# Two of the seven half products of a weight tile summed by TensorE in one PSUM bank instead of by VectorE

## The chip, the cores and the metric

The kernel runs on one core of a Trainium2 chip. A core has five engines that each run their own queue of instructions in order: TensorE (PE, with its weight loads as PEld) for matmuls, VectorE (DVE), ScalarE (ACT), GpSimd (POOL) and SyncE (SP), which only starts transfers. They wait for each other by semaphores. Matmuls write into PSUM, which has eight banks; a bank holds 128 x 512 numbers in fp32. The metric is the device time of one execution in microseconds (us), lower is better; three runs of the kernel before gave 1572.64 to 1574.14 with a median of 1573.52.

## The reference

One block works on 512 latent tokens and 256 context tokens of 1024 channels: a SwiGLU feed-forward network (FFN), a token mixer, and a second FFN on the latent tokens alone. The change touches only the first matrix product of the two FFNs, `u @ wi`.

```
def swiglu(u, wi, wo):
    gate, up = jnp.split(u @ wi, 2, axis=-1)
    return (jax.nn.silu(gate) * up) @ wo

def ffn_half(t, m, s, nw, wi, wo):
    u = modulate(t, nw, m[3 * s], m[3 * s + 1])
    return t + 0.5 * m[3 * s + 2] * swiglu(u, wi, wo)
...
h = ffn_half(h, lat_m, 0, norm_w[l, 0], ffn1_wi[l], ffn1_wo[l])
hc = ffn_half(hc, ctx_m, 0, norm_w[l, 0], ffn1_wi[l], ffn1_wo[l])
...
h = ffn_half(h, lat_m, 2, norm_w[l, 2], ffn2_wi[l], ffn2_wo[l])
```

`wi` is 1024 x 5632 (two times 2816 hidden channels), all in fp32. The kernel splits each operand into a high part of reduced precision and the rest (names ending in h and l) and adds three matmuls, high times high, high times low and low times high.

## The kernel before, in words

A weight tile of `wi` is 1024 rows by 256 hidden channels. Its product with the tokens is cut in halves along all three sides, which would be eight products of half size, and is computed with seven (Strassen's scheme in Winograd's form): seven combinations of weight quarters times seven combinations of token quarters, and additions that put the four quarters of the result together. One call of `half_gemm` does this for one weight tile, with a column count N of 384 in the first FFN (768 tokens) and 256 in the second. In this document such a call is a **round**. A product is 12 matmuls (four blocks of 128 rows, three matmuls each) into one PSUM bank, so a round is 84 matmuls. Products are numbered 0 to 6 in their order.

Hidden channels are done in pairs of 128 (`half_pair`): a **gate round**, whose quarters go through Silu on ScalarE into the tiles `s`, and then an **up round**, whose quarters are multiplied into `s` by VectorE (line 1157); the finished `s` is split into `ah` and `al` (lines 76 and 77 in `split`) for the second matrix product. There are 20 rounds in the first FFN (from about 79 to 549 us) and 20 in the second (from about 1226 to 1523 us), numbered 1 to 40 here; odd rounds are gate rounds, even ones up rounds. The first pair of hidden channels of each FFN is done in another way.

After some pairs the second matrix product (`down`, the matmuls of line 229) is done for the hidden channels collected so far. It stands between the gate round and the up round of the next pair, so it cuts the rounds into **blocks**: rounds 1 to 3, 4 to 7, 8 to 11, 12 to 13, 14 to 17 and 18 to 20 in the first FFN, 21 to 27, 28 to 35 and 36 to 40 in the second.

What happens around a round:

- Weights come by DMA into `raw`; GpSimd forms four sums of weight quarters (`ws`, line 247: s3, s1, s2 and the fourth); each of the seven operands is split into `wh` by a cast on ScalarE and `wl` by a subtraction on VectorE. They go through a ring of 6 slots (8 in the second FFN), so a weight is prepared 6 or 8 products ahead, when a product sets a slot free.
- Product 0 is copied from its bank into SBUF by ScalarE (tile `hu`, line 307). VectorE then does seven additions (line 296), each of one bank and one tile in SBUF: product 0 plus product 1 is quarter (0,0) of the result; `hu` plus product 4, and so on for the other three quarters.
- The token operands are the normed tokens (`u_hi`, `ul_hi` and the like) and four sums of them, `T0` to `T3`.
- Every engine's order is fixed when the program is built: a scheduler orders the instructions by its own estimate of when each can run. On the chip an instruction that waits holds up all that stand behind it on its engine.

In the first FFN VectorE and ScalarE also do parts of another computation between the products (lines 511 to 600, the modulation by `w_ada`).

Of the kernel before, what the change touches and what calls it, by code (L numbers as in the profile page):

```python
# [12 lines left out]
AF = mybir.ActivationFunctionType  # L13
# [22 lines left out]
class Block:  # L36
# [203 lines left out]
    def half_items(self, w, r0, c0):  # L240

        nc, st = self.nc, {}
        a = lambda k, m: st["raw"][k][:, :, m * P : (m + 1) * P]

        def sub(x, y, op=ALU.subtract):
            t = self.sp.tile([P, 4, P], F32, tag="ws", name=self.n("ws"), bufs=self.sums)
            nc.gpsimd.tensor_tensor(out=t, in0=x, in1=y, op=op)  # L247
            return t

        def make(i):  # L250
            if i == 0:
                st["raw"] = self.load_raw([(w, r0, c0, 256)], KT)
                s3 = sub(a(0, 0), a(0, 1))
                s1 = sub(a(0, 1), a(1, 1), ALU.add)
                s2 = sub(s1, a(0, 0))
                st["w"] = [a(0, 0), a(1, 0), s3, sub(a(1, 0), s2), s2, a(1, 1), s1]
            src = st["w"][i]
            h, l = (t.rearrange("p (k n) -> p k n", k=4) for t in self.ring())
            self.split(h, l, src)
            return h, l  # L260

        return [(1, lambda i=i: make(i)) for i in range(7)]

    def half_operands(self, u):

        o = lambda k, t: lambda kt: u(k, t, kt)
        v = lambda j: lambda kt: self.T[j][kt]
        self.hx = [o(0, 0), o(1, 0), v(2), o(1, 1), v(1), v(3), v(0)]

    def half_sums(self, kt, x0, x1, last=None):  # L270

# [19 lines left out]
    def half_gemm(self, N, out, fill):  # L291

        nc = self.nc
        banks = []
        t = self.tmp.tile([P, N], F32, tag="hu", name=self.n("hu"), bufs=2)
        add = lambda o, x, y: nc.vector.tensor_tensor(out=o, in0=x, in1=y, op=ALU.add)  # L296
        for i in range(7):
            h, l = self.next_w()
            ps = self.small()[:, :N]
            banks.append(ps)  # L300
            for kt in range(4):
                xh, xl = self.hx[i](kt)
                for j in range(3):
                    nc.tensor.matmul(ps, (h, h, l)[j][:, kt, :], (xh, xl, xh)[j], start=kt == 0 and j == 0, stop=kt == 3 and j == 2)  # L304
            self.done_w()
            if i == 0:
                nc.scalar.copy(t, ps)
            elif i == 1:
                c = out(0, 0)
                add(c, t, ps)  # L310
                out(0, 0, c)
            elif i == 4:
                add(t, t, ps)
                c22, c12 = out(1, 1), out(0, 1)
                add(c22, t, banks[2])
                add(c12, t, banks[3])
            elif i == 5:
                c = out(1, 0)
                add(c, c22, ps)
                out(1, 0, c)  # L320
            elif i == 6:
                add(c12, c12, ps)
                out(0, 1, c12)
                add(c22, c22, ps)
                out(1, 1, c22)
            fill(i)
# [787 lines left out]
    def ffn(self, i, first, tail, fillers, after, between, tail_pool):  # L1114

        nc = self.nc
        ctx = i == 0
        W = TOK if ctx else SEQ
        N = W // 2
        bufs = max(k1 - k0 for k0, k1 in self.parts[i])  # L1120
        fill = lambda: next(fillers, None)
        acts, held = [], []

        def silu():
            return self.tmp.tile([P, W], F32, tag="s", name=self.n("s"), bufs=2 if ctx else 3)

        def keep(s):
            acts.append([self.act.tile([P, W], F32R, tag="a" + k, name=self.n("a" + k), bufs=bufs) for k in "hl"])
            self.split(*acts[-1], s)

        def evac_gate(pg):
            s = silu()
            for k, g in zip((0, SEQ), pg):
                w = min(SEQ, W - k)
                self.last_silu = nc.scalar.activation(s[:, k : k + w], g[:, :w], AF.Silu)
            return s

        def evac_up(s, pu):
            for k, u in zip((0, SEQ), pu):
                w = min(SEQ, W - k)  # L1140
                c = s[:, k : k + w]
                nc.vector.tensor_tensor(out=c, in0=c, in1=u[:, :w], op=ALU.mult)
            keep(s)

        def half_pair(m):
            ss = [silu(), silu()]
            at = lambda i, j: ss[i][:, j * N : (j + 1) * N]

            def gate(i, j, c=None):
                if c is not None:  # L1150
                    self.last_silu = nc.scalar.activation(c, c, AF.Silu)
                return at(i, j)

            def up(i, j, c=None):
                if c is None:
                    return self.tmp.tile([P, N], F32, tag="c", name=self.n("c"), bufs=3)
                nc.vector.tensor_tensor(out=at(i, j), in0=at(i, j), in1=c, op=ALU.mult)  # L1157
                if j == 1:
                    keep(ss[i])

            every = (1, 4) if m > 4 or not ctx else range(m == 2, 7)
            self.half_gemm(N, gate, lambda j: fill() if j in every and m > 2 else None)
            if held:
                held.pop()()
            self.half_gemm(N, up, lambda j: fill() if j in every else None)

        def down(acts, group, each, then=None):

            nk = len(acts)
            segs = []  # L1170
            for s, t0, w in group:
                sl = slice(s * SEQ + t0, s * SEQ + t0 + w)
                segs.append((sl.start, w, lambda kt, sl=sl: (acts[kt][0][:, sl], acts[kt][1][:, sl])))
            for t in range(4):
                w_ = self.next_w()
                os = [self.wide(W) for _ in range(2)]
                if t == 0:
                    self.gemm([(o, w_, j * P, P) for j, o in enumerate(os)], segs, nk)
                    if ctx and then:
                        then()  # L1180
                for j, o in enumerate(os):
                    m = 2 * t + j
                    if t:
                        self.gemm([(o, w_, j * P, P)], segs, nk)
                    for s, t0, w in group:
                        h = (self.h_l, self.h_c)[s][:, m, t0 : t0 + w]
                        nc.vector.scalar_tensor_tensor(out=h, in0=o[s][:, t0 : t0 + w], scalar=self.hg[:, s, m : m + 1],  # L1187
                                                       in1=h, op0=ALU.mult, op1=ALU.add)
                        each(m, s, t0, w)
                    fill()  # L1190
                self.done_w()
                if t == 0 and then and not ctx:
                    then()

        for k0, k1 in self.parts[i]:
            for m in range(k0, k1, 2):
                if m == 0:
                    first(evac_gate, evac_up)
                else:
                    half_pair(m)  # L1200
            if k1 < HM:
                held.append(lambda acts=tuple(acts): down(acts, [(0, 0, SEQ)] + ([(1, 0, CTX)] if ctx else []), lambda *k: None))
                acts.clear()
        for _ in fillers:
            pass
        self.log_exp(self.last_silu)
        tail_pool()
        then = None
        for group in tail:
            down(acts, [group], after, then)  # L1210
            then = lambda group=group: between(*group)
        then()
# [826 lines left out]
```

## Time and profile before

| | |
|---|---|
| median of three runs | 1573.52 us |
| the profiled execution, its own time | 1573.72 us |
| its span (first to last instruction) | 1571.9 us, so 1.8 us lie around it |
| mean granted TensorE clock | 0.994 |
| TensorE busy | 98% of the span |
| VectorE busy | 78% |
| ScalarE busy | 50% |
| GpSimd busy | 18% |

The spans and waits come from one profiled execution. A busy share is a mean over all stages; which engine is waited for in a stage is read from the waits and the timeline of that stage. The end of a matmul is modelled by the profiler, its start is measured.

### The profile page before, as it was taken

Reading aid. Unit: us, or ns where it says so; the run is one execution under the profiler, and the core shown is the slowest. Engines: PE = TensorE matmul, PEld = TensorE weight load, DVE = VectorE, ACT = ScalarE, POOL = GpSimd, SP = SyncE. Lnnn points to the kernel's source line nnn. Section 1 sums busy time; section 2 is a strip of 40 time slices with the busy share of each in tenths; the row PEclk is TensorE's granted clock in tenths of the full one; section 3 lists DMA queues with packets and bytes.
Section 4 is the critical chain, followed back from the end, with each engine's and each line's share of the span. In section 5 each row is a group of like instructions: output and inputs, shape, how many; then the busy total and the mean of one; then the engine's idle time right before and its main releaser. Section 6 shows DMA issues by size and latency. Waiting matters only on the chain. (4 is left out here: it accounts for less than half of the span.)

```text
span 1571.9 us, 24897 instructions
## 1 busy us (share of the span) xinstructions
PE 1536.4 (98%) x9292; PEld 1378.4 (88%) x9292; DVE 1229.4 (78%) x2230; ACT 779.4 (50%) x1363; POOL 281.8 (18%) x222
## 2 busy tenths in 40 slices
PE   8989999999999999999999999999999999999997
PEld 4778998999998988899898888878899898998997
DVE  5897999989996797776577577777756996797695
ACT  6754242433252456355353487778335643444365
POOL 0121212311312130000000100000013442451322
PEclk9999999999999999999999999999999999999999
DMA  9225334342443233121216223223531234234233
GB/s 329 89 68 154 101 115 128 112 137 66 136 128 94 81 105 108 41 58 52 66 54 188 74 61 93 68 81 121 174 108 55 68 104 125 81 95 132 83 116 113
DMA packets 165076, 163.63 MB, mean 104 GB/s; under 512 B 7618, under 2 KB 162524, under 8 KB 164956
## 3 DMA queue, kind: packets, MB, share of 16 engines
q1 hardware_dynamic: 163932, 159.68, 33.5%
q0 software_dynamic: 1024, 2.36, 0.5%
q8 instruction: 73, 1.20, 0.3%
q14 instruction: 47, 0.39, 0.1%
HBM read 159.89 MB, written 2.10 MB: 103 GB/s over the span
## 5 line engine op out<-in xcount | busy, mean ns | idle before, releaser
L76 ACT CAST wh<-raw 128x512 fp32r<-128x512 f32 x396 | 239.9, 618 | 240.6 <-PE sm L229 96.4
L77 DVE TENSOR_TENSOR wl<-raw,wh 128x512 fp32r<-128x512 f32 x396 | 288.7, 740 | 85.4 <-ACT wh L76 83.0
L229 PE MATMUL sm<-al,wh 128*128 128x512 f32 (+1 forms) x576 | 172.8, 340 | 0.1
L229 PE MATMUL sm<-ah,wh 128*128 128x512 f32 (+1 forms) x576 | 172.7, 342 | 0.0
L229 PE MATMUL sm<-ah,wl 128*128 128x512 f32 (+1 forms) x576 | 172.2, 339 | 0.0
L76 ACT CAST wh<-ws 128x512 fp32r<-128x512 f32 x160 | 97.9, 618 | 135.1 <-PE sm L229 65.5
L229 PE MATMUL mm<-ul_lo,wh 128*128 128x512 f32 x352 | 141.7, 402 | 0.0
L229 PE MATMUL mm<-ul_hi,wh 128*128 128x512 f32 x352 | 140.9, 400 | 0.0
L229 PE MATMUL mm<-ul_hi,wl 128*128 128x512 f32 x352 | 139.9, 397 | 0.0
L77 DVE TENSOR_TENSOR wl<-ws,wh 128x512 fp32r<-128x512 f32 x160 | 126.1, 799 | 10.9 <-ACT wh L76 10.6
L523 DVE SCALAR_TENSOR_TENSOR acc<-apiece,cs,acc 128x256 f32<-128x256 f32 x224 | 121.8, 567 | 14.9 <-DMA apiece<-in_w_ada_dram 12.6
L247 POOL TENSOR_TENSOR ws<-raw 128x512 f32<-128x512 f32 x40 | 61.1, 1529 | 357.8 <-DVE wl L77 141.0
L229 PEld LDWEIGHTS sm<-al,wh 128*128 128x128 f32 x576 | 98.5, 189 | 13.0 <-DVE al L77 0.3
L229 PEld LDWEIGHTS sm<-ah,wh 128*128 128x128 f32 x576 | 98.4, 188 | 12.9 <-ACT ah L76 0.3
L229 PEld LDWEIGHTS sm<-ah,wl 128*128 128x128 f32 x576 | 98.5, 189 | 12.8
L304 PE MATMUL sm<-u_lo,wh 128*128 128x384 f32 x320 | 108.0, 337 | 1.6 <-DVE u_lo L77 1.6
L304 PE MATMUL sm<-u_hi,wh 128*128 128x384 f32 x320 | 107.8, 337 | 0.1
L304 PE MATMUL sm<-u_hi,wl 128*128 128x384 f32 x320 | 107.8, 337 | 0.0
L1187 DVE SCALAR_TENSOR_TENSOR h_l<-sm,hg,h_l 128x512 f32<-128x512 f32 (+1 forms) x80 | 55.0, 692 | 44.3 <-PE sm L229 44.1
L1599 POOL DMA_DIRECT2D gwr<-in_lru_wr_dram x8 | 5.8, 726 | 417.2 <-PE mm L229 294.6
L229 PEld LDWEIGHTS mm<-ul_hi,wh 128*128 128x128 f32 x352 | 66.3, 188 | 15.8 <-issue 0.5
L229 PEld LDWEIGHTS mm<-ul_hi,wl 128*128 128x128 f32 x352 | 66.3, 188 | 15.3
(496 smaller groups left out, 4258.0 us busy)
## 6 DMA issues: line engine op xcount, KB each, us to landing
raw<-in_ffn_wi_dram SPq DMA_DIRECT2D x84, 512.0 KB
apiece<-in_w_ada_dram SPq DMA_DIRECT2D x112, 256.0 KB
raw<-in_ffn_wo_dram SPq DMA_DIRECT2D x48, 512.0 KB
raw<-in_w_in_dram SPq DMA_DIRECT2D x48, 512.0 KB
araw<-in_w_ada_dram SPq DMA_DIRECT2D x8, 1024.0 KB
raw<-in_w_in_dram SPq DMA_DIRECT2D x16, 256.0 KB
raw<-in_w_out_gla_dram SPq DMA_DIRECT2D x8, 512.0 KB
raw<-in_w_out_lru_dram SPq DMA_DIRECT2D x8, 512.0 KB
```

Of the source, the lines that this page charges most:

```text
L76: nc.scalar.copy(hi, src)
L77: rest = lambda: (nc.gpsimd if eng == "p" else nc.vector).tensor_tensor(out=lo, in0=src, in1=hi.bitcast(F32), op=ALU.subtract)
L229: ins = nc.tensor.matmul(dst[:cols, d0 : d0 + width], wk, xs, start=(kt == 0 and i == 0 and not (shared and n)), stop=(kt == kts - 1 and i ...
L247: nc.gpsimd.tensor_tensor(out=t, in0=x, in1=y, op=op)
L304: nc.tensor.matmul(ps, (h, h, l)[j][:, kt, :], (xh, xl, xh)[j], start=kt == 0 and j == 0, stop=kt == 3 and j == 2)
L523: nc.vector.scalar_tensor_tensor(out=acc[:, s, :], in0=raw[:, kt, :], scalar=c, in1=acc[:, s, :], op0=ALU.mult, op1=ALU.add)
L1187: nc.vector.scalar_tensor_tensor(out=h, in0=o[s][:, t0 : t0 + w], scalar=self.hg[:, s, m : m + 1], in1=h, op0=ALU.mult, op1=ALU.add)
L1599: nc.gpsimd.dma_start(out=raw[:, 0:2, :], in_=self.a["lru_wr"][0, :, blk].rearrange("d c e -> c d e"))
```

## The change

Products 1 and 2 change places: the sum s3 times T2 is now product 1, and the product of weight quarter (1,0) with token quarter (1,0), which was product 1, is now product 2. Product 2 doesn't start a bank of its own. Its matmuls add onto product 0 in that product's bank (`banks[0]`, no `start`), after ScalarE has copied product 0 to `hu`. The bank then holds quarter (0,0), which `out` takes straight from PSUM: in a gate round ScalarE's Silu reads the bank, in an up round VectorE's multiplication does. The addition of `i == 1` is gone, and six remain. A round now takes six banks from the pool instead of seven.

```
@@ half_items
-                st["w"] = [a(0, 0), a(1, 0), s3, sub(a(1, 0), s2), s2, a(1, 1), s1]
+                st["w"] = [a(0, 0), s3, a(1, 0), sub(a(1, 0), s2), s2, a(1, 1), s1]
@@ half_operands
-        self.hx = [o(0, 0), o(1, 0), v(2), o(1, 1), v(1), v(3), v(0)]
+        self.hx = [o(0, 0), v(2), o(1, 0), o(1, 1), v(1), v(3), v(0)]
@@ half_gemm
         for i in range(7):
             h, l = self.next_w()
-            ps = self.small()[:, :N]
+            ps = banks[0] if i == 2 else self.small()[:, :N]
             banks.append(ps)
             for kt in range(4):
                 xh, xl = self.hx[i](kt)
                 for j in range(3):
-                    nc.tensor.matmul(ps, (h, h, l)[j][:, kt, :], (xh, xl, xh)[j], start=kt == 0 and j == 0, stop=kt == 3 and j == 2)
+                    nc.tensor.matmul(ps, (h, h, l)[j][:, kt, :], (xh, xl, xh)[j], start=kt == 0 and j == 0 and i != 2,
+                                     stop=kt == 3 and j == 2, skip_group_check=i == 2)
             self.done_w()
             if i == 0:
                 nc.scalar.copy(t, ps)
-            elif i == 1:
-                c = out(0, 0)
-                add(c, t, ps)
-                out(0, 0, c)
+            elif i == 2:
+                out(0, 0, ps)
             elif i == 4:
                 add(t, t, ps)
                 c22, c12 = out(1, 1), out(0, 1)
-                add(c22, t, banks[2])
+                add(c22, t, banks[1])
                 add(c12, t, banks[3])
@@ half_pair, gate
-                    self.last_silu = nc.scalar.activation(c, c, AF.Silu)
+                    self.last_silu = nc.scalar.activation(at(i, j), c, AF.Silu)
```

The first place to look at is TensorE's order where product 2 begins, here in round 34 (an up round of the second FFN). `ul` are the tokens, `T2` the second token sum, the numbers tell tiles apart. Before, `sm_2901` is the bank of product 0, `sm_2904` that of product 1 and `sm_2908` that of product 2:

```order
L304 MATMUL sm_2904_14977<-ul_hi_6011,wh_2874_14828 128x256
L304 MATMUL sm_2904_14977<-ul_lo_6012,wh_2874_14828 128x256
L304 MATMUL sm_2904_14977<-ul_hi_6011,wl_2875_14829 128x256
L304 MATMUL sm_2908_14997<-T20h_12340,wh_2877_14846 128x256 [waits DVE_49,Activation_49]
L304 MATMUL sm_2908_14997<-T20l_12341,wh_2877_14846 128x256
L304 MATMUL sm_2908_14997<-T20h_12340,wl_2878_14847 128x256
```

Now `sm_2852` is the bank of product 0 and `sm_2855` that of product 1:

```order
L304 MATMUL sm_2855_14895<-T23h_12296,wh_2826_14748 128x256
L304 MATMUL sm_2855_14895<-T23l_12297,wh_2826_14748 128x256
L304 MATMUL sm_2855_14895<-T23h_12296,wl_2827_14749 128x256
L304 MATMUL sm_2852_14877<-ul_hi_5961,wh_2829_14766 128x256 [waits Activation_49]
L304 MATMUL sm_2852_14877<-ul_lo_5962,wh_2829_14766 128x256
L304 MATMUL sm_2852_14877<-ul_hi_5961,wl_2830_14767 128x256 [waits DVE_49]
```

Product 2 goes back to the bank of product 0, and its first matmul waits for ScalarE (Activation), which has to have read that bank. In seven of the 40 rounds the scheduler puts one or five matmuls of product 3 ahead of product 2; in the first three rounds and in round 21, where products of several banks are mixed, the mixture changes too. On SP's queue the same transfers stand, with those of weights and of `w_ada` interleaved differently in the first FFN.

The second place is ScalarE's order around the copy of product 0 in the same round. `s_2870` and `s_2871` are the Silu tiles of the gate round just before, `wh` are casts of weights for later products. Before:

```order
L1151 ACTIVATE s_2870_14812<-s_2870_14812 128x256 [waits DVE_49]
L76 CAST wh_2883_14882<-ws_2862_14792 128x512 [waits PE_49,Activation_49]
L76 CAST wh_2886_14899<-raw_2859_14786 128x512 [waits PE_49,Activation_49]
L76 CAST wh_2889_14919<-ws_2861_14790 128x512 [waits PE_49,Activation_49]
L1151 ACTIVATE s_2871_14813<-s_2871_14813 128x256 [waits DVE_49,Activation_49]
L76 CAST wh_2898_14950<-raw_2892_14938 128x512 [waits DMAHW0_49,PE_49]
L1151 ACTIVATE s_2870_14812<-s_2870_14812 128x256 [waits DVE_49]
L1151 ACTIVATE s_2871_14813<-s_2871_14813 128x256 [waits DVE_49]
L76 CAST wh_2902_14972<-raw_2893_14940 128x512 [waits DMAHW1_49,PE_49]
L307 COPY hu_2900_14958<-sm_2901_14959 128x256 [waits PE_49]
```

Now, with the line numbers of the changed kernel (Silu at 1150, the copy at 308):

```order
L1150 ACTIVATE s_2822_14732<-sm_2825_14735 128x256 [waits PE_49]
L76 CAST wh_2834_14800<-ws_2814_14712 128x512 [waits PE_49,Activation_49]
L76 CAST wh_2837_14817<-raw_2811_14706 128x512 [waits PE_49,Activation_49]
L76 CAST wh_2840_14837<-ws_2813_14710 128x512 [waits PE_49,Activation_49]
L1150 ACTIVATE s_2823_14733<-s_2823_14733 128x256 [waits DVE_49,Activation_49]
L76 CAST wh_2849_14868<-raw_2843_14856 128x512 [waits DMAHW0_49,PE_49]
L1150 ACTIVATE s_2822_14732<-s_2822_14732 128x256 [waits DVE_49]
L1150 ACTIVATE s_2823_14733<-s_2823_14733 128x256 [waits DVE_49]
L76 CAST wh_2853_14890<-ws_2845_14860 128x512 [waits PE_49,Pool_49]
L308 COPY hu_2851_14876<-sm_2852_14877 128x256 [waits PE_49]
```

The first Silu no longer waits for VectorE but for TensorE. The copy keeps its place behind the three Silus that wait for VectorE's additions of the round before, and the cast just ahead of it now waits for GpSimd's sum instead of a DMA. In gate rounds the copy stands behind one or both casts `ah<-s`, which wait for VectorE's multiplications, in both kernels.

The third place is VectorE's order at the same point. Before, the addition into `c_2907` is the one that goes, `hu_2900` is the copied product 0:

```order
L77 TENSOR_TENSOR wl_2903_14973<-raw_2893_14940,wh_2902_14972 128x512 [waits DMAHW1_49,PE_49,Activation_49]
L296 TENSOR_TENSOR c_2907_14994<-hu_2900_14958,sm_2904_14977 128x256 [waits PE_49,Activation_49]
L1157 TENSOR_TENSOR s_2870_14812<-s_2870_14812,c_2907_14994 128x256 [waits DVE_49]
L77 TENSOR_TENSOR wl_2906_14991<-ws_2894_14942,wh_2905_14990 128x512 [waits Activation_49]
L77 TENSOR_TENSOR wl_2910_15011<-ws_2897_14948,wh_2909_15010 128x512 [waits PE_49,Activation_49]
L77 TENSOR_TENSOR wl_2913_15028<-ws_2896_14946,wh_2912_15027 128x512 [waits PE_49,Activation_49]
L296 TENSOR_TENSOR hu_2900_14958<-hu_2900_14958,sm_2914_15031 128x256 [waits PE_49]
```

Now:

```order
L77 TENSOR_TENSOR wl_2857_14909<-raw_2844_14858,wh_2856_14908 128x512 [waits DMAHW1_49,PE_49,Activation_49]
L1156 TENSOR_TENSOR s_2822_14732<-s_2822_14732,sm_2852_14877 128x256 [waits PE_49]
L77 TENSOR_TENSOR wl_2859_14925<-ws_2848_14866,wh_2858_14924 128x512 [waits Activation_49]
L77 TENSOR_TENSOR wl_2862_14943<-ws_2847_14864,wh_2861_14942 128x512 [waits PE_49,Activation_49]
L296 TENSOR_TENSOR hu_2851_14876<-hu_2851_14876,sm_2863_14946 128x256 [waits PE_49]
```

The multiplication now reads the bank itself and waits for product 2 instead of product 1, and the next two splits and the addition of product 4 stand behind it.

## Rows read from the trace of the kernel before

**Rows 1.** The profile page, busy time, share of the span and instructions of each engine

```profile
PE 1536.4 (98%) x9292; PEld 1378.4 (88%) x9292; DVE 1229.4 (78%) x2230; ACT 779.4 (50%) x1363; POOL 281.8 (18%) x222
```

**Rows 2.** Busy time by stretch: length, PE, PEld, DVE, ACT, POOL, clock, DMA, GB/s

```profile
160.00:325.00 165.00, 165.00 (x962) 157.67 (x961) 160.58 (x297) 59.23 (x105) 40.82 (x28) 1.00 0.39 116
...
1225.00:1315.00 90.00, 85.22 (x633) 81.09 (x632) 85.68 (x145) 45.21 (x96) 33.76 (x22) 0.96 0.34 104
1350.00:1430.00 80.00, 80.00 (x673) 79.91 (x672) 76.61 (x130) 42.45 (x85) 36.56 (x23) 1.00 0.35 106
```

**Rows 3.** TensorE's waits, whole span: total us, times, longest

```profile
PE sm L304 <- ACT wh L76: 3.0, 1, 3.0
PE sm L304 <- DVE hu L296: 2.8, 3, 1.9
```

**Rows 4.** Groups by line and form: busy us, mean ns, idle before, releaser

```profile
L1157 DVE TENSOR_TENSOR s<-s,c 128x256 f32<-128x256 f32 x40 | 21.9, 555 | 0.3
...
L296 DVE TENSOR_TENSOR s<-hu,sm 128x384 f32<-128x384 f32 x30 | 15.6, 546 | 0.0
...
L296 DVE TENSOR_TENSOR s<-hu,sm 128x256 f32<-128x256 f32 x30 | 12.0, 412 | 0.3
...
L1151 ACT ACTIVATE s<-s 128x256 f32<-128x256 f32 x40 | 15.8, 418 | 30.5 <-DVE s L296 30.5
...
L76 ACT CAST ah<-s 128x512 fp32r<-128x512 f32 x22 | 13.3, 620 | 35.2 <-DVE s L1157 35.2
```

**Rows 5.** Timeline of round 34: start, duration, engine, line, idle before

```profile
1413.24 0.28 PE L304 MATMUL sm<-T20h,wh 128*128 128x256 f32 x1
...
1415.86 0.42 ACT L1151 ACTIVATE s<-s 128x256 f32<-128x256 f32 x1 [3.21 <-DVE s L296]
...
1416.29 0.74 DVE L296 TENSOR_TENSOR s<-s,sm 128x256 f32<-128x256 f32 x2
...
1416.73 0.75 ACT L1151 ACTIVATE s<-s 128x256 f32<-128x256 f32 x2
...
1417.89 0.36 ACT L307 COPY hu<-sm 128x256 f32<-128x256 f32 x1
```

**Rows 6.** Timeline, rounds 7, 11, 13, 15, 26, 39: product 2, copy of product 0

```profile
226.21 0.34 PE L304 MATMUL sm<-T20h,wh 128*128 128x384 f32 x1
230.10 0.47 ACT L307 COPY hu<-sm 128x384 f32<-128x384 f32 x1
...
319.62 0.34 PE L304 MATMUL sm<-T20h,wh 128*128 128x384 f32 x1
323.93 0.47 ACT L307 COPY hu<-sm 128x384 f32<-128x384 f32 x1
...
384.10 0.34 PE L304 MATMUL sm<-T20h,wh 128*128 128x384 f32 x1
385.96 0.47 ACT L307 COPY hu<-sm 128x384 f32<-128x384 f32 x1
...
430.96 0.34 PE L304 MATMUL sm<-T20h,wh 128*128 128x384 f32 x1
433.45 0.47 ACT L307 COPY hu<-sm 128x384 f32<-128x384 f32 x1
...
1288.65 0.28 PE L304 MATMUL sm<-T20h,wh 128*128 128x256 f32 x1
1294.63 0.36 ACT L307 COPY hu<-sm 128x256 f32<-128x256 f32 x1
...
1507.14 0.28 PE L304 MATMUL sm<-T20h,wh 128*128 128x256 f32 x1
1508.87 0.36 ACT L307 COPY hu<-sm 128x256 f32<-128x256 f32 x1
```

**Rows 7.** TensorE after its longest wait for VectorE: timeline, then busy by stretch

```profile
1257.38 0.36 PE L304 MATMUL sm<-ul_hi,wh 128*128 128x256 f32 x1 [1.86 <-DVE hu L296]
...
1259.10:1262.20 3.10, 3.10 (x15) 3.10 (x16) 3.10 (x8) 0.00 (x0) 1.28 (x1) 0.50 0.56 150
```

## The prediction

> **What bounds the kernel now.** The busy time by engine comes first: TensorE is busy 1536.4 us of the span, VectorE 1229.4 [rows 1]. That suggests TensorE and little to win elsewhere, so I look next at the stretches in which the rounds run [rows 2]. TensorE has no idle time from 160 to 325 us and from 1350 to 1430 us, but VectorE is busy 160.58 of 165 us and 76.61 of 80 us there: both engines are near full, and TensorE is the one that ends last. A product of 12 matmuls takes 165.00 / 962 x 12 = 2.06 us in the first FFN and 80.00 / 673 x 12 = 1.43 us in the second.
>
> TensorE's waits say how often the half products stand for VectorE's additions: 2.8 us in three waits in the whole span [rows 3]. The additions are thus off the path nearly everywhere. But ScalarE does wait for VectorE: its Silus 30.5 us for line 296 in the second FFN alone, the casts `ah` 35.2 us for line 1157 [rows 4]. VectorE runs behind TensorE, and ScalarE hangs on VectorE.
>
> The timeline of round 34 shows how far behind [rows 5]. Product 2 starts at 1413.24. ScalarE has stood 3.21 us for an addition of the gate round before, does a Silu at 1415.86, the last two Silus at 1416.73 when VectorE's two additions are done (1416.29 + 0.74 = 1417.03 for the later one; the first of the Silus can start on the first), and copies product 0 only at 1417.89 to 1418.25. That is 5.01 us after product 2 began. Today nobody minds: product 2 goes to another bank, and the addition that reads `hu` stands behind the same backlog on VectorE.
>
> **What the change removes.** 40 additions: 20 of 0.546 us and 20 of 0.412 us [rows 4], 10.9 + 8.2 = 19.1 us of VectorE's time. None of it is TensorE's, so it counts only as far as VectorE is waited for. As a saving by itself it can bring at most the 2.8 us of rows 3.
>
> **What it adds.** Product 2 writes the bank that ScalarE's copy reads, so TensorE stops at product 2 until the copy is done, and products 3 to 6 stand behind it. The cover is product 1, 2.06 or 1.43 us. The copy has not moved in ScalarE's order: it still stands behind Silus or `ah` casts that wait for VectorE. So the price is the copy's lateness, end of the copy minus start of product 2. TensorE doesn't pay it anew in each round: once it has stood, it is later by that much against VectorE's backlog, which runs on through the stop. What counts is the largest lateness in each block, because `down` between blocks gives VectorE time to catch up. From rows 5 and 6:
>
> - rounds 4 to 7, at round 7: 230.10 + 0.47 - 226.21 = 4.36
> - rounds 8 to 11, at round 11: 323.93 + 0.47 - 319.62 = 4.78
> - rounds 12 and 13, at round 13: 385.96 + 0.47 - 384.10 = 2.33
> - rounds 14 to 17, at round 15: 433.45 + 0.47 - 430.96 = 2.96
> - rounds 21 to 27, at round 26: 1294.63 + 0.36 - 1288.65 = 6.34
> - rounds 28 to 35, at round 34: 5.01
> - rounds 36 to 40, at round 39: 1508.87 + 0.36 - 1507.14 = 2.09
>
> Together 27.9 us; the two blocks not named have almost none.
>
> **What comes off.** The additions removed earlier in the same block shorten the backlog: 3, 3, 1 and 1 in the four blocks of the first FFN, 5, 6 and 3 in the second, 8 x 0.546 + 14 x 0.412 = 10.2 us. That would leave 17.7. But VectorE gets a stop of its own. In up rounds the multiplication now waits for product 2 instead of product 1, with two weight splits and the next addition behind it (the order above), and once TensorE has waited for the copy, VectorE waits there for a whole product, 1.43 us or more, with only splits in hand to fill part of it. No row of before shows this wait. Its bounds are nothing given back and all given back, 17.7 and 27.9; I take the middle, 22.8, as up rounds are half of all.
>
> **The clock.** After the longest wait for VectorE, 1.86 us idle, the granted clock read 0.50 from 1259.10 to 1262.20, the lower of the two levels, which cost half of 3.10 us, 1.55 [rows 7]. That is the only price here for a stop of such a size. Three blocks of the first FFN have stops of 2 us or more left (rounds 4 to 7, 8 to 11, 14 to 17), so 3 x 1.55 = 4.7; below none, above one in each of the seven blocks, 10.9. Rounds 21 to 27 have that stop and its price in their time already.
>
> **The moved product.** Product 1 now needs `T2` one product earlier, 2.06 us at the first round and 1.43 at round 21, where those sums are only just made, so up to 3.5 us, and nothing at best. I count 0: in the first FFN a wait of 3.0 us for a weight cast comes later in the start and takes the shift up [rows 3], and the second start runs at VectorE's pace. s3's split moves one place ahead too, in front of the copy and behind GpSimd's sum; with casts 6 to 8 products ahead of use I count 0, and its worst is in the upper end. On SP's queue the same transfers are issued, those of weights and of `w_ada` in the first FFN in another interleaving; the DMA engines are busy 0.39 of that stretch [rows 2], so I count that at 0 too, and a late weight would again be in the upper end.
>
> **One rule.** A multiplication of line 1157 takes 0.555 us on average for 256 columns, an addition that reads a bank 0.412 [rows 4]. The Trainium skill (SBUF — State Buffer, section Who interferes with whom) says that a VectorE instruction with two inputs in SBUF contends with GpSimd's reads, and one with a single SBUF input does not; the two means agree. The ten multiplications of the second FFN that now read a bank would by this rule save 10 x 0.143 = 1.4 us of VectorE, and the sum would be 1.4 lower at the most.
>
> **Sum.** 22.8 + 4.7 = 27.5 us. On the profiled execution's 1573.72 us that is 1601.2; the median of the runs lies 0.2 us lower, so I say **1601**. Its own range is 17.7 + 0 to 27.9 + 10.9: 1591 to 1612.
>
> **Rivals.**
>
> *Lockstep.* TensorE and VectorE wait for each other in every pair, the backlog is rebuilt each time, and each late copy costs the clock as well. In the trace 20 of the 40 copies are late by 1.86 us or more, seven of which are shown [rows 5, 6]: 27.9 + 20 x 1.55 = 58.9, some 1633. For it: VectorE's new wait. Against: after a first stop the later ones should be short, about a microsecond a pair. The Trainium skill (TensorE: Matmul & The Clock Gate, section HAM oscillation — how this bites in real kernels) describes kernels in which waits between groups of matmuls bring the clock down again and again; rows 7 agree for one such wait, and by that rule this rival is what happens.
>
> *A small loss.* The backlog of before is largely that of the removed additions and of copies that stand behind them by the scheduler's choice; with 10.2 us off in full, and the moved Silu no longer stopping ScalarE, lateness falls below 2 us in most blocks: about 8 us in all, 1582.
>
> *Faster.* VectorE's relief brings all copies inside the cover of product 1. Then the 2.8 us that TensorE waits for the additions and the 1.55 us of clock behind them go, 1573.5 - 4.4 = 1569. It takes over when 10.2 us of relief make up for 27.9 of lateness, and with five of seven largest values above 2.9 us I see nothing that does.
>
> *No change.* The wait is there but something holds TensorE at the same places anyway. The second stretch with no idle time at all [rows 2] speaks against it.
>
> **How the numbers follow.** This kernel's measurement can tell 0.2%, 3.1 us, from no change. Chances: forecast 0.63, lockstep or the ground between 1612 and it 0.15, small loss 0.13, no change 0.04, faster 0.05. Left out below 1583 are faster, no change and half of the small loss, above 1618 some two thirds of lockstep: about 0.2 together, so 1583 to 1618. Faster 0.05, same 0.04, slower 0.91.
>
> **What would show it.** TensorE's waits list ScalarE's copy `hu` at line 308 or its equivalent with 20 us or more, in single waits of up to 4 us; the rounds' stretches have idle TensorE time where there was none; VectorE's busy time is some 19 us lower; the copy's place behind Silus and casts that wait for VectorE is as before; the granted clock dips to 0.5 behind the longest stops. The prediction is wrong if the copies come within the time of product 1, or if VectorE stands at the multiplication of product 2 for much longer than a product.

## The result and the profile after

The changed kernel takes 1597.43 us, median of five runs, the kernel before 1572.64 in the same session, so 24.8 us are lost. The ratio on record is 1.0166, with a 95% interval of 1.0155 to 1.0177 (these two medians alone give 1.0158). The profiled execution of the changed kernel took 1598.16 us, 24.4 more than that of before (1573.72). The loss is in the forecast range, and 3.6 us smaller than the forecast.

The page's busy time by engine, after, answers to [rows 1]:

```profile
PE 1543.2 (97%) x9292; PEld 1381.1 (87%) x9292; DVE 1218.1 (76%) x2190; ACT 784.6 (49%) x1363; POOL 286.1 (18%) x222
```

VectorE has 40 instructions fewer, and yet only 11.3 us less busy time, not 19.1; the section on the prediction comes back to this. TensorE has the same 9292 matmuls and needs longer. Its waits after answer to [rows 3] (total us, times, longest):

```profile
PE sm L304 <- ACT hu L308: 19.5, 15, 7.7
...
PE sm L304 <- ACT wh L76: 2.4, 1, 2.4
PE sm L304 <- ACT T22h L76: 1.9, 1, 1.9
```

The waits for VectorE's additions `hu` are gone, 2.8 us before. ScalarE's copy (line 308 now) has taken their place with 19.5 us. The stretches of [rows 2], after:

```profile
160.00:325.00 165.00, 159.94 (x906) 151.39 (x905) 153.52 (x280) 56.62 (x100) 41.04 (x28) 0.98 0.37 112
1225.00:1315.00 90.00, 79.77 (x626) 77.61 (x624) 83.28 (x150) 48.75 (x101) 36.85 (x22) 0.94 0.25 78
1350.00:1430.00 80.00, 77.51 (x567) 73.07 (x566) 65.92 (x98) 35.63 (x68) 41.80 (x27) 1.00 0.30 91
```

TensorE had no idle time in the first and the third of them, and now stands 5.06 and 2.49 us there; VectorE, which was nearly full, has idle time too. The timeline, cut to ScalarE and to the matmul that waited, shows the wait in round 7 (first five rows) and in round 24 (the rest):

```profile
227.94 0.83 ACT L76 CAST ah<-s 128x768 fp32r<-128x768 f32 x1 [4.04 <-DVE s L1156]
228.68 0.61 ACT L76 CAST wh<-ws 128x512 fp32r<-128x512 f32 x1
229.20 0.47 ACT L308 COPY hu<-sm 128x384 f32<-128x384 f32 x1
...
229.72 0.44 PE L304 MATMUL sm<-u_hi,wh 128*128 128x384 f32 x1 [2.07 <-ACT hu L308]
...
1283.34 0.42 ACT L1150 ACTIVATE s<-s 128x256 f32<-128x256 f32 x1 [4.83 <-DVE s L296]
1283.66 0.60 ACT L76 CAST wh<-ws 128x512 fp32r<-128x512 f32 x1
1284.21 0.42 ACT L1150 ACTIVATE s<-s 128x256 f32<-128x256 f32 x1
1284.54 0.35 ACT L308 COPY hu<-sm 128x256 f32<-128x256 f32 x1
...
1284.94 0.58 PE L304 MATMUL sm<-ul_hi,wh 128*128 128x256 f32 x1 [7.70 <-ACT hu L308]
```

Read each piece upwards. TensorE waits for the copy; the copy itself waits for nothing of its own, as product 0 was done long before; it stands behind an `ah` cast or a Silu that waits for VectorE. Product 2 starts 0.05 us after the copy's end in both. ScalarE is busy 49% of the span, and the copy is late only by its place in the queue.

The clock after the stops, by stretch (columns as in rows 2):

```profile
230.00:234.00 4.00, 4.00 (x16) 4.00 (x16) 3.08 (x7) 1.68 (x4) 0.00 (x0) 0.57 0.11 33
298.00:302.00 4.00, 4.00 (x16) 4.00 (x15) 2.26 (x4) 1.32 (x3) 3.08 (x2) 0.57 0.47 138
...
1285.00:1289.00 4.00, 4.00 (x21) 4.00 (x22) 2.19 (x4) 1.33 (x3) 2.85 (x2) 0.57 0.39 130
...
443.00:447.00 4.00, 4.00 (x24) 4.00 (x25) 3.51 (x5) 2.11 (x4) 2.48 (x1) 1.00 0.46 133
...
1256.00:1275.00 19.00, 19.00 (x157) 18.46 (x156) 19.00 (x29) 6.48 (x14) 10.45 (x7) 1.00 0.34 103
```

Three stops (2.07, 1.74 and 7.70 us) are followed by a granted clock partly at the lower level, 0.57 on the mean of 4 us each time: 3 x 0.43 x 4.00 = 5.2 us. The 2.09 us stop in round 15, which ended at 442.89, is followed by 1.00. The last row is the place where before had its longest wait for VectorE and its own slow clock [rows 7]: 19 us without idle time at full clock, so 1.86 + 1.55 = 3.4 us come back there.

Where the time goes is plainest from the start of each round, the same matmul in the program of each kernel, read from the traces. This table is worked out: start in the kernel named less start in the kernel before, in us, and in the last two columns the last matmul of round 40 and the end of the span. The experiments' rows are used below. They hold one execution each, from other sessions, in which before took 1570.8 to 1571.6 us and not 1573.72; e16 below, which takes the same time as before by the medians, would end 3.2 us early in this table. So jumps within a row are read from it, and not ends of rows of that size.

```
round             4     8    12    14    18    21    24    28    36   last   end
changed        -0.5   5.2   9.9   9.7  12.8  13.0   9.4  18.3  22.9   24.7  24.4
e12_dummy_add  -0.1   5.7   8.9   8.3  13.4  13.7  10.3  20.6  28.4   32.9  32.5
e1_swap_only   -0.3   0.6   0.4   0.3   0.3   0.3   0.9   1.9   6.4    6.3   8.7
e2_relief_only -1.8  -1.8  -1.9  -2.6  -2.6  -2.6  -5.3  -6.4  -6.4   -6.4  -6.8
e4_fourth       0.7   1.0   0.9   0.9   1.4  -0.3   0.6   3.4   4.4    4.4   4.4
e8_late_both   -1.1   4.4   6.2   5.7   6.9   5.3   1.7   5.7   5.8    5.7   5.5
e15_all_late   -0.4   0.9   0.8   0.1   0.1   0.1  -3.5  -1.2  -1.2   -1.3  -1.6
```

In the changed kernel 13.0 us are lost in the first FFN, nothing between the start of round 20 and that of round 21 (547 and 1239 us), and 11.7 in the second.

### The profile page after: what moved, and what is told of

It is laid out like the page before. It is cut to its first block, busy times and chain, and to the rows that moved or that the text cites. A ratio compares the mean times of both kernels' runs of the same rounds, so it can differ in the third digit from the quotient of the medians.

```text
span 1596.4 us, 24684 instructions
## 1 busy us (share of the span) xinstructions
PE 1543.2 (97%) x9292; PEld 1381.1 (87%) x9292; DVE 1218.1 (76%) x2190; ACT 784.6 (49%) x1363; POOL 286.1 (18%) x222
## 5 line engine op out<-in xcount | busy, mean ns | idle before, releaser
L229 PEld LDWEIGHTS sm<-ah,wl 128*128 128x128 f32 x576 | 98.3, 188 | 12.7
L304 PE MATMUL sm<-ul_hi,wh 128*128 128x256 f32 x240 | 70.5, 294 | 11.7 <-ACT hu L308 11.3
L247 POOL TENSOR_TENSOR ws<-raw,raw 128x512 f32<-128x512 f32 x40 | 56.6, 1414 | 139.7 <-DVE wl L77 60.6
```

The source lines that it names most:

```text
L229: ins = nc.tensor.matmul(dst[:cols, d0 : d0 + width], wk, xs, start=(kt == 0 and i == 0 and not (shared and n)), stop=(kt == kts - 1 and i ...
```

## The experiments

Theory: the loss is the time by which ScalarE's copy is late, and it is late because it stands behind instructions that wait for VectorE. Rivals: the new order of the products costs by itself; coming back to a bank costs whenever it is done; VectorE is late whatever ScalarE does. Times are medians, and ratios are against runs of the kernel before on the same chip (1570.8 to 1571.6 us).

**The order alone.** `e1_swap_only`:

```
-            ps = banks[0] if i == 2 else self.small()[:, :N]
+            ps = self.small()[:, :N]
...
             elif i == 2:
-                out(0, 0, ps)
+                c = out(0, 0)
+                add(c, t, ps)
+                out(0, 0, c)
```

> The order of the products of the changed kernel (A = a00 first, then s3 with T2, then a10), but a10's product has its own bank and its addition on VectorE, as before; so 280 banks, seven additions, no wait of TensorE for the copy. Theory (the loss is the wait of product 2 for the copy of product 0): 1573 us, 1571 to 1576, and no wait of TensorE for the copy. Rival (the loss is the moved product: T2 and s3 one place earlier, the other interleaving on SP's queue): 1590 us or more.

1581.74 us, 1.0066 (1.0054 to 1.0079): neither the theory's number nor the rival's. The first FFN loses 0.3 us by the table, so T2 and s3 a place earlier cost nothing there. The loss is in the second FFN, and it isn't at T2 either. TensorE's waits in this kernel:

```profile
PE sm L304 <- DVE s L296: 3.3, 3, 2.2
PE sm L304 <- DVE hu L296: 3.3, 4, 2.3
```

and its longest one by the timeline, with the stretch behind it:

```profile
1417.83 0.36 PE L304 MATMUL sm<-ul_hi,wh 128*128 128x256 f32 x1 [2.24 <-DVE s L296]
```

```profile
1417.80:1422.00 4.20, 4.17 (x22) 4.14 (x23) 4.17 (x8) 1.89 (x5) 0.98 (x1) 0.61 0.04 5
```

2.24 us and 0.39 of 4.20 us of clock are 3.9 us, most of the 4.5 us from round 28 to 36; 1.6 us before that and 2.4 behind the last round were not looked into. The first addition now comes one product later and, behind VectorE's backlog, frees its bank too late. Read from the trace, not tested: this is a price of the order with the addition kept. The changed kernel has no such addition, and e15 below shows that it doesn't pay this price.

**The relief alone.** `e2_relief_only`, from the kernel before; it leaves product 0 out of quarter (0,0), so its result isn't the block's:

```
             elif i == 1:
-                c = out(0, 0)
-                add(c, t, ps)
-                out(0, 0, c)
+                out(0, 0, ps)
```

> The kernel before with the first addition of each round left out and nothing in its place: product 1 goes to its own bank and its quarter takes that bank alone, so product 0 is missing from quarter (0,0). It is the relief of VectorE alone, 40 additions, without any wait. Theory (VectorE is off the path before, so that its relief is worth at most the 2.8 us of waits for it and 1.55 us of clock): 1569 to 1573 us. Rival (the relief is worth much and the changed kernel's copies cost all the more): 1560 us or less.

1567.12 us, 0.9973 (0.9962 to 0.9984): 3.8 us gained for 19.1 us of additions removed. The time itself is 1.9 us below the range given, which was reckoned from 1573.5; against before on this chip (1570.95) the gain keeps the theory's bound of 2.8 + 1.55 us. Before, the additions were off the path but for a few waits.

**The removed work put back, the wait kept.** `e12_dummy_add`:

```
             elif i == 2:
                 out(0, 0, ps)
+                add(out(0, 1), t, ps)
```

> The changed kernel with the removed addition put back on VectorE as work alone: it reads hu and the shared bank behind product 2 and writes a tile that is overwritten or not read, so that VectorE has before's 40 additions and TensorE still waits for the copy. Theory of the sum (the relief takes 5.1 us, at most 10.2 us, off the lateness): 1602 us, 1600 to 1609. Rival (the relief brings the changed kernel nothing, since VectorE waits for TensorE's product in any case): 1596 to 1599 us.

1605.51 us, 1.0218 (1.0202 to 1.0234), 8.1 us more than the changed kernel. Its waits for the copy, and the clock behind four of its stops:

```profile
PE sm L304 <- ACT hu L308: 24.4, 14, 6.5
...
214.50:218.50 4.00, 3.92 (x15) 3.92 (x16) 4.00 (x8) 1.77 (x5) 1.29 (x1) 0.61 0.39 133
442.80:446.80 4.00, 4.00 (x16) 4.00 (x15) 2.56 (x5) 1.38 (x3) 2.65 (x2) 0.57 0.44 137
1296.90:1303.10 6.20, 6.20 (x29) 6.20 (x30) 5.47 (x7) 2.51 (x5) 3.72 (x3) 0.50 0.25 78
1528.00:1532.00 4.00, 4.00 (x21) 4.00 (x22) 3.45 (x5) 1.04 (x2) 2.89 (x2) 0.57 0.41 135
```

The waits are 24.4 - 19.5 = 4.9 us longer, close to the theory's 5.1. The clock takes 1.6 + 1.7 + 3.1 + 1.7 = 8.1 us where it took 5.2, so 2.9 more; together 7.8 of the 8.1 us. VectorE's relief does shorten the copies' lateness, and the rival, no relief at all, is out. The addition stands one product later here than before the change, so this is the nearest kernel and not the exact one.

**More cover.** `e3_third` and `e4_fourth` move the product that is summed one and two places later; for `e4_fourth`:

```
-                st["w"] = [a(0, 0), s3, a(1, 0), sub(a(1, 0), s2), s2, a(1, 1), s1]
+                st["w"] = [a(0, 0), s3, sub(a(1, 0), s2), s2, a(1, 0), a(1, 1), s1]
...
-            ps = banks[0] if i == 2 else self.small()[:, :N]
+            ps = banks[0] if i == 4 else self.small()[:, :N]
```

> The changed kernel with a10's product one place later: order a00, s3, s4, a10, s2, a11, s1, still summed in product 0's bank. The copy has two products of cover in place of one. Theory (what counts is the lateness of the copy over its cover): each block's lateness falls by one product, 2.06 or 1.43 us, so that of 23.7 us about 12.7 stay, and with one dip of the clock 1586 us, 1580 to 1590. Rival (it is the return to a bank that another engine has read that costs, whenever it comes): 1595 us or more.

1592.9 us, 1.0135 (1.0120 to 1.0151): less than the changed kernel, and between the theory's range and the rival's. The waits for the copy fell from 19.5 to 17.6 us only, in 12 places, and rounds 30 to 34 stop five times for 6.1 us together (starts of matmuls), where the changed kernel stops for 3.5. Part of it may be that a shorter stop in one round leaves TensorE further ahead of VectorE in the next. Two waits are new: 2.0 us for a multiplication (line 1156) and 1.7 for a Silu, which both now read their quarter one product later. Why the waits fall so little stays open.

> The changed kernel with a10's product two places later: order a00, s3, s4, s2, a10, a11, s1. The copy has three products of cover. Theory of lateness over cover: 5.7 us stay in the block of rounds 21 to 27, about one in rounds 28 to 35 and nothing elsewhere: 1579 us, 1573 to 1583. Rival (the return to the bank costs whenever it comes): 1595 us or more.

1578.34 us, 1.0044 (1.0030 to 1.0057), as forecast. The first FFN loses 1.4 us now instead of 13.0. TensorE's waits:

```profile
PE sm L304 <- ACT hu L308: 3.9, 4, 1.5
```

The bank that is come back to is the same; with three products of cover the wait is nearly gone. So it isn't the return to the bank that costs. The Trainium skill (Perfetto Trace Analysis, section Matmuls) wants independent groups of matmuls to take different banks, so that one bank is emptied while the next group runs; the trace agrees, if the count is made for the bank that is reused here: 19.5 us of waits with one group between, 3.9 with three.

**T2 at its old place.** `e10_s4_first` has the same three products of cover with another order:

```
-                st["w"] = [a(0, 0), s3, a(1, 0), sub(a(1, 0), s2), s2, a(1, 1), s1]
+                st["w"] = [a(0, 0), sub(a(1, 0), s2), s3, s2, a(1, 0), a(1, 1), s1]
```

> The changed kernel with the order a00, s4, s3, s2, a10, a11, s1: three products of cover for the copy, as in the order a00, s3, s4, s2, a10, a11, s1 that ran at 1578.3, but T2 is used where it was before the change. Theory (cover takes the wait away, and what was left of 7.4 us were sums at the start of the second FFN, 3.0 us for T2 alone, while the relief of VectorE by itself brings 4): 1572 us, 1568 to 1577. Rival (what was left is the price of reading product 0's bank so late, or of additions that come later): 1578 us or more.

1578.34 us, 1.0042 (1.0029 to 1.0055): the median of `e4_fourth` again. That is the rival's side: the theory's gain from T2's place did not come. `T22h` is waited for 1.5 us less than in `e4_fourth`, but for `wh` 1.0 longer, with some shorter waits beside it.

**The copy's place in the queue.** `e7_late_silu` holds back the last three Silus of a gate round until the next round's copy is issued, `e8_late_both` the `ah` casts of an up round too:

```
             if i == 0:
-                nc.scalar.copy(t, ps)
+                self.flush(nc.scalar.copy(t, ps))
...
+    def flush(self, ins=None):
+        self.behind = ins
+        for f in self.late:
+            f()
+        self.late, self.behind = [], None
...
+                def go():
+                    self.last_silu = nc.scalar.activation(at(i, j), c, AF.Silu)
+                    if self.behind is not None:
+                        self.after(self.last_silu, self.behind)
                 if c is not None:
-                    self.last_silu = nc.scalar.activation(at(i, j), c, AF.Silu)
+                    self.late.append(go) if i or j else go()
```

> The changed kernel with the last three Silus of each gate round put behind the next up round's copy in ScalarE's queue (an order within the engine, no new wait on another one). Theory (the copy is late because it stands behind ScalarE instructions that wait for VectorE): the stops of the up rounds, 13.6 of the 23.7 us, go, those of the gate rounds, behind ah casts, stay or grow a little; 1582 us, 1578 to 1589. Rival (the copy is late for ScalarE's own work or for the bank, so that its place behind Silus doesn't matter): 1595 us or more.

1594.52 us, 1.0150 (1.0134 to 1.0166), far from the theory and half a microsecond short of the rival's 1595. The stops of the up rounds did shrink, in round 24 from 7.86 us to 2.39 by the starts of matmuls, but round 25 stops for 4.16 instead of 0.26. The late Silus wait 4.06 us for VectorE where they stand now, and the next copy stands behind them and behind an `ah` cast that waits 3.87 us for VectorE's multiplications: what one copy no longer waits for, the next one does.

> As the kernel with late Silus, and the two ah casts of each up round are put behind the next gate round's copy too, so that no copy stands behind an instruction that waits for VectorE's products of the round before. Theory: all 23.7 us of stops and the clock behind them go: 1572 us, 1567 to 1578, with less than 3 us of waits for the copy. Rival (VectorE is too late in any case, so that the wait only moves from the copy to the additions or the free banks): 1588 us or more.

1580.39 us, 1.0058 (1.0044 to 1.0073): 17.0 us less than the changed kernel and between the two expectations. The waits for the copy are 10.8 us, and the timeline of round 7 (ScalarE, and the matmul) says why:

```profile
227.25 0.83 ACT L76 CAST ah<-s 128x768 fp32r<-128x768 f32 x1 [4.74 <-DVE s L1174]
227.99 0.61 ACT L76 CAST wh<-ws 128x512 fp32r<-128x512 f32 x1
228.51 0.47 ACT L318 COPY hu<-sm 128x384 f32<-128x384 f32 x1
...
229.03 0.69 PE L314 MATMUL sm<-u_hi,wh 128*128 128x384 f32 x1 [2.84 <-ACT hu L318]
```

The copy still stands behind an `ah` cast: this kernel holds the casts back within a block but not past its last round, so the expectation's "no copy" was untrue at the ends of blocks. By the starts of rounds its loss in the first FFN grows by 4.6, 1.8 and 1.2 us in rounds 7, 11 and 17, the last before a block ends at `down`, and by 1.0 in round 6.

`e15_all_late` holds them back there too:

```
-            self.split(*acts[-1], s)
+            if late:
+                self.late.append(lambda a=acts[-1]: self.split(*a, s))
+            else:
+                self.split(*acts[-1], s)
```

> The changed kernel with its own order of products, and now every ah cast of a round behind the next round's copy too, those at the ends of blocks among them, which the kernel with both late had left in front (its stops of 3.0 us in round 7 and its shifts at rounds 11 and 17 stand there). Theory (the copy's place in ScalarE's queue is the whole price): some 5 to 6 us less than the 1580.4 us of that kernel, 1575 us, 1571 to 1578, with less than 6 us of waits for the copy. Rival (VectorE is late whatever ScalarE does, and the stops only move): 1579 us or more.

1572.18 us, 1.0002 (0.9993 to 1.0010): no loss is left. TensorE's waits, and ScalarE's timeline of round 7 (first two rows) and of round 24 with the matmul that waits:

```profile
PE sm L314 <- ACT hu L318: 4.4, 3, 2.1
```

```profile
225.57 0.47 ACT L318 COPY hu<-sm 128x384 f32<-128x384 f32 x1
...
228.33 0.83 ACT L76 CAST ah<-s 128x768 fp32r<-128x768 f32 x1 [2.28 <-DVE s L1177]
...
1261.55 1.14 ACT L76 CAST ah<-s 128x512 fp32r<-128x512 f32 x2 [7.15 <-DVE s L1177]
...
1265.98 0.36 ACT L318 COPY hu<-sm 128x256 f32<-128x256 f32 x1
...
1266.40 0.39 PE L314 MATMUL sm<-ul_hi,wh 128*128 128x256 f32 x1 [2.07 <-ACT hu L318]
```

In round 7 the copy is done at 226.04, inside product 1, and the cast that waits for VectorE stands behind it. In round 24 it is late still, since the casts of an earlier round keep ScalarE waiting for 7.15 us and six weight casts and a Silu come before the copy. This kernel has the changed kernel's order of products, bank, additions and instructions. ScalarE has 74 of its 1363 instructions at other places; VectorE has 19 and TensorE 7, which the scheduler moved too. 25.3 us are gone.

**Is the late order a gain of its own?** `e16_before_late` is the kernel before with the same late Silus and casts.

> The kernel before, its seven banks, seven additions and its order of products, with the same late Silus and ah casts as in the kernel with all late (1572.2 us). It tells how much the late order brings by itself. Theory (the copy is not waited for in the kernel before, so that its place is worth nothing there, and the late order took away the changed kernel's wait and nothing else): 1570 to 1574 us, the same as before. Rival (the late order is a gain of its own that paid for a loss the sum of banks still has): 1568 us or less.

1571.08 us, 1.0000 (0.9991 to 1.0009): worth nothing there. TensorE doesn't wait for the copy in the kernel before, and its place is free.

**Both remedies.** `e14_s4_third_late` and `e13_s4_first_late` join the late order with two and three products of cover.

> All of it late as in the kernel before this one in the list, and the order of products a00, s4, s3, a10, s2, a11, s1, still summed in product 0's bank: two products of cover, and T2 and T1 at their places of before. Theory: no waits for the copy left, and the relief of 40 additions of 4 us shows: 1569 us, 1565 to 1574, which would be no slower than before. Rival (s4's place and the later additions cost by themselves): 1576 us or more.

1570.90 us, 1.0000 (0.9990 to 1.0009), in the range, but with 4.3 us of waits for the copy where none were expected.

> As the kernel with a10's product in the fourth place, but in the order a00, s4, s3, s2, a10, a11, s1 with three products of cover. It ran at 1578.3 us without the late casts and Silus, with 4.4 us of waits for the copy. Theory: these 4.4 us go and little else, 1573 us, 1568 to 1576. Rival (what was left has to do with banks and additions and not with the copy): 1577 us or more.

1572.37 us, 1.0006 (0.9997 to 1.0015), with 2.0 us for the copy and 1.9 for an addition. No version that computes the block beats the kernel before. The few waits that stay, 3.9 to 4.4 us in these two and in e15, are as large as the 3.8 us that the relief is worth by itself; that they are what uses it up is likely, and not shown.

## Why the prediction was right, step by step

- **The mechanism held.** The copy took the additions' place among TensorE's waits, behind the instructions that were named, and e15, with e16 beside it, shows that its place in ScalarE's queue is the price but for the 4.4 us of waits that stay in e15.
- **The lateness of each block** was a good measure, with some luck. Growth of the shift over rounds 4 to 7, 8 to 11, 12 and 13, 14 to 17, 21 to 27, 28 to 35, 36 to 40, clock included: 5.7, 4.7, -0.2, 3.1, 5.3, 4.6, 1.8 us, against lateness of 4.36, 4.78, 2.33, 2.96, 6.34, 5.01, 2.09. Only rounds 12 and 13 missed: two rounds, with one wait of 0.22 us in them. That the rest fits so closely is partly chance, since growth has the clock in it and lateness doesn't have the relief taken off. e12, where VectorE has its additions, is the cleaner check: 24.4 us of waits against 27.9 of lateness.
- **The relief came out near its size, but not for its reason.** The sum let half of 10.2 us count, 5.1; by e12 the waits are 4.9 us shorter with it. The reason for halving it was a stop of VectorE at the moved multiplication of a product or more. That stop is small: line 1156 waits 3.9 us for TensorE, in five places, and not 1.43 us or more in every pair. The addition `hu` waits 10.7 us in 20 places, 1.0 at the longest. So the middle of the two bounds was a lucky choice.
- **The clock was near in sum, for other places, which is luck too.** Forecast were three dips in the first FFN, 4.7 us. Measured are two there and one in round 24, 5.2 us, but the one of before at 1259 us is gone, so 3.6 net. The 2.09 us stop in rounds 14 to 17 had none. The sum also left out that the 2.8 us of waits for the additions go [rows 3]. With these, 27.9 - 4.9 + 3.6 - 2.8 = 23.8 of the 24.4 us measured; 0.6 us were not assigned.
- **The moved product at 0 held** in the changed kernel: the shift is -0.5 us at round 4 and unchanged from 20 to 22, T22h is waited for once, 1.9 us (0.5 before), and the wait for `wh` is 0.6 shorter. By e1 the moved place does cost when the addition is kept, which the prediction had no need of.
- **The one rule** on multiplications that read a bank: line 1156 by the duration of its forms, from the trace of the changed kernel (ns, least, median, largest):

```profile
L1156 DVE TENSOR_TENSOR s<-s,c x60: 409/545/1515, 119.5 to 1550.4; 128x384 f32<-128x384 f32 x30, 128x256 f32<-128x256 f32 x30
L1156 DVE TENSOR_TENSOR s<-s,sm x20: 406/478/555, 112.2 to 1543.6; 128x384 f32<-128x384 f32 x10, 128x256 f32<-128x256 f32 x10
```

  Reading the bank, none takes over 555 ns; reading two tiles of SBUF, up to 1515. The ten that read a bank with 256 columns take 0.413 us on average, before 0.555, so the rule's 1.4 us of VectorE came. With 384 columns, in the first FFN, neither kind takes over 0.56 us. The Trainium skill (SBUF — State Buffer, section Who interferes with whom) says the same of which forms can be held up.
- **Three signs were off.** The waits for the copy are 19.5 us, just under the "20 us or more". "Single waits of up to 4 us": round 24's is 7.7. Before, TensorE waited for an addition in round 23 and paid the clock, 3.4 us, and its copy of round 24 was 5.0 us late; the addition is gone, TensorE arrives 3.3 us earlier (the shift falls from 12.7 at round 23 to 9.4 at 24), and the stop is 2.7 us longer than that lateness. And VectorE's busy time fell by 11.3 instead of 19 us. The durations of its instructions, added up from the two traces, did fall by 19.9 us (1366.2 to 1346.3). But neighbours overlap in the records, by some 0.08 us where they follow each other at once, and busy time counts an overlap once, so it shows less than was removed.
- **The rivals.** Lockstep's text counts 20 of the 40 copies as late by 1.86 us or more; the trace of before has 18. It did not come: 15 waits, and three slow clocks. The small loss (1582) wanted lateness below 2 us in most blocks, and four blocks lost 4.6 us or more. No change came only with another order on ScalarE, and faster with none that was tried and computes the block.

## What to carry to other kernels

Before matmuls add onto a bank that another engine must first read, look where that read stands in its engine's queue, not at how busy the engine is: here a 0.4 us copy on an engine that is half idle cost 25 us, because it stood behind instructions that wait for a third engine. The lateness of the read in the trace of before, end of the read minus start of the matmul that will need it, taken as the largest of each stretch, gave the loss within a few us. The remedies are the order of the reading engine's queue or more groups of matmuls in between, and what saved work is worth is bounded by the waits for it, not by its duration: before the change 2.8 us and the clock behind them, against 19.1. Once TensorE waits for an engine that hangs on the saved work, it counts for more: the same additions put back cost the changed kernel 8.1 us.

## What the runs showed of the hardware

A stop's length alone did not tell whether the clock fell: 2.07 and 1.74 us were followed by a clock partly at the lower level, 2.09 us by 1.00.

The same VectorE instruction takes 0.69 or 1.78 us in one trace, by what GpSimd does meanwhile. From the timeline of e1_swap_only, VectorE's `al` and GpSimd's instructions:

```profile
1411.60 1.79 POOL L247 TENSOR_TENSOR ws<-raw,raw 128x512 f32<-128x512 f32 x1 [2.45 <-DMA raw<-in_ffn_wi_dram]
...
1412.16 1.78 DVE L77 TENSOR_TENSOR al<-s,ah 128x512 fp32r<-128x512 f32 x1
...
1413.47 1.63 POOL L247 TENSOR_TENSOR ws<-ws,raw 128x512 f32<-128x512 f32 x1
...
1416.06 0.69 DVE L77 TENSOR_TENSOR al<-s,ah 128x512 fp32r<-128x512 f32 x1
...
1417.50 1.29 POOL L247 TENSOR_TENSOR ws<-raw,ws 128x512 f32<-128x512 f32 x1 [2.40 <-DVE wl L77]
```

The first `al` runs beside GpSimd's sums, the second while GpSimd is idle (from 1415.10 to 1417.50). Of the 22 such splits in this trace, the 14 during which GpSimd is idle all the time take 0.675 to 0.694 us. So how fast VectorE works off a backlog depends on when GpSimd runs.
